# A two-layer encoder: the second layer's output projection as seven products of quarters

## The chip, the core and the metric

The kernel runs on one NeuronCore of a Trainium2 chip. Its time is the device time of one execution, in microseconds, as the median of several runs. A core has a matrix engine (PE, with its weight loads as PEld), a vector engine (DVE), a scalar engine (ACT), a general engine (POOL) and a queue engine (SP); SP, ACT and POOL issue DMAs. Each engine works through its own list of instructions in the order of that list.

## The reference

A trunk of two layers over 512 tokens of width 1024, all in float32. Each layer is a mixer with a gated branch, a residual add, and a gated per-layer embedding; layer 0's mixer is attention over a neighbourhood, layer 1's is dense attention with low-rank queries and keys. Cut to what matters here:

```python
def mixer_mla(xn, w_in, q_norm, w_qb, kv_norm, w_kvb, w_out):
    ...
    o = block_attention(q, k, v)
    return (o.reshape(B, S, H * MLA_V) * jax.nn.silu(z)) @ w_out

def reference(x, p, ...):
    for i in range(DEPTH):
        xn = rmsnorm(x, norm_g[i])
        ...
        h = x + y
        gate = jax.nn.sigmoid(rmsnorm(h, ple_norm[i]) @ ple_w_gate[i])
        x = h + gate * (p[i] @ ple_w_proj[i])
    return rmsnorm(x, final_norm)
```

The change is about `(o * silu(z)) @ w_out` and `h = x + y` of layer 1: 512 x 1024 times 1024 x 1024.

## The kernel before

**Precision.** Every float32 operand of a product is kept as two parts, a rounded `hi` (an ACT copy) and the remainder `lo` (a subtraction on POOL or DVE), and a product is hi·hi + lo·hi + hi·lo: three matmuls of 128 rows, 128 columns of stationary operand and up to 512 moving columns. A weight piece is 128 x 1024; `load_w` (L72) loads it into one of three `wraw` buffers on SP's queue, and makes `hi` and `lo` of it.

**Stages.** The first layer's attention (`na_heads`, L224), its output projection and gate; then the second layer's compression (`mla_c`, L669) with its gate projections z (`z_phase`, L164: eight weights, each 24 matmuls, `Silu` into the eight tiles `zs`), its heads (`mla_heads`, L717), its output projection (`out_proj`, L414) and its gate (`gate_seven`, L564). The loop in `run` (L1009) does projection and gate of both layers.

**Heads.** A loop of 70 steps i, four to a head, interleaves on PE: the scores of step i (`score`), whose softmax goes over DVE, ACT and POOL; the transposes of step i-3 (`turn`); the products with the values of a head before (`output`); and pieces of work for later (`pieces`, L856), among them the per-layer embedding's products (`ple`, L896), 16 calls of 3 matmuls, whose results are stored on SP. When a pair of heads j is done, `half_of` joins it (DVE, L205) and `gated` (L207) multiplies by `zs[j]` (POOL, L209) and splits the result into `oT`, the projection's operand.

**The output projection.** `out_proj` loads eight pieces of `mla_o`; per column half n and row tile t, 24 matmuls add up in one PSUM bank; DVE adds it to the residual row (L427), and `turn_h` (L1023) then scales the row (`hg`, DVE, L1028), transposes it (PE) and gives it to `keep_half` (L536), which makes operands X of the gate's products. The residual rows (`r`, from `spill`) and the norm's gains (`gp`) are read at the beginning of this stage. The framework may place its matmuls from step 53 of the heads on.

**The gate, already from seven products.** `gate_seven` cuts both operands in quarters (256 tokens x 512 features, 512 x 512 weights) and forms 7 products instead of 8, each of two row tiles and 12 matmuls. Sums of quarters of the weights are formed in DRAM by `sum_step` (L518), eight DMAs of 1 MB a layer on POOL's queue, every second one of which adds onto what is there; they are issued one a head during the first layer's attention. The last product, 4, is done in halves of 256 columns at the end.

**Order.** The framework orders each engine's instructions when the program is built, by its own model of their durations, in which the order of the program text is the priority; `issue_after(x)` puts an instruction behind x on the same engine. A buffer pool hands out a tile when an old one's last reader is done. PSUM has eight banks here (tags mm 2, S 2, T 3, O 1, L67).

## Time and profile before

| | us |
|---|---|
| median of 3 runs | 661.84 (661.47 to 661.88) |
| the profiled execution | 662.75 |
| its span, first to last instruction | 660.6 |

The mean granted clock of TensorE in it was 0.997. The rows in the next section are of that one execution: a line of code, an engine, an operation, what it writes and reads, how often, and either start and duration (timelines), or total and mean (groups); in brackets the idle time before it and what ended that. In a row of a stretch the first number is its length, and each engine's busy time follows. The chain is the work that ended last, followed back.

### The profile page before, as it was taken

What the parts mean: (1) busy time and instruction counts of PE and PEld (TensorE: products, weight loads), DVE (VectorE), ACT (ScalarE), POOL (GpSimd) and SP (SyncE); (2) the same over time, 40 slices, a digit from 0 to 9 for tenths busy, and PEclk for the clock granted to TensorE, in tenths of its full rate; (3) what the DMA queues carried; (4) which work ended last, traced back from release to release, by engine and by line L of the source; (5) the groups of instructions that cost most, each with busy time, mean ns of one, the idle gap of its engine ahead of it and who ended that gap; (6) DMA issues with size and microseconds to landing.
All of it is one profiled execution on the core that took longest, in us unless ns stands there. A gap on an engine that the chain in (4) does not pass through costs nothing.

```text
span 660.6 us, 10121 instructions
## 1 busy us (share of the span) xinstructions
PE 648.1 (98%) x3419; PEld 550.8 (83%) x3419; DVE 403.3 (61%) x856; ACT 439.4 (67%) x875; POOL 432.5 (65%) x381
## 2 busy tenths in 40 slices
PE   9999999999999999999999999999999999999994
PEld 6888888988988888887899888888888888888884
DVE  6190365836546526568833623888888876474865
ACT  7672586856767743787643535888979897537945
POOL 0495485686685674687555525795959878436974
PEclk9999999999999999999999999999999999999998
DMA  9944357886587779445733344220211213584524
GB/s 326 346 144 147 96 168 190 221 201 143 172 218 173 199 172 372 161 132 167 250 90 105 106 109 141 65 75 3 64 56 65 66 59 133 202 308 128 166 90 159
DMA packets 44755, 102.18 MB, mean 155 GB/s; under 512 B 4640, under 2 KB 17696, under 8 KB 44704
## 3 DMA queue, kind: packets, MB, share of 16 engines
q1 hardware_dynamic: 33776, 83.97, 38.3%
q0 software_dynamic: 10496, 16.78, 11.8%
q10 hardware_dynamic: 432, 0.79, 0.3%
q8 instruction: 27, 0.44, 0.3%
q14 instruction: 24, 0.20, 0.1%
HBM read 89.99 MB, written 25.17 MB: 174 GB/s over the span
## 4 chain that ended last, share of the span: by engine, by line
PE 87%; DVE 3%; DMA 3%; POOL 2%; ACT 2%; issue 2%; POOLq 0%; ACTq 0%; DVEq 0%
PE ps_mm L107 33%; PE ps_S L107 13%; PE ps_mm L734 6%; PE ps_T L139 5%; PE ps_O L845 4%; PE ps_T L637 4%; PE ps_T L107 3%; PE ps_O L107 3%; PE ps_T L238 2%; PE ps_S L637 2%; PE ps_O L400 2%; PE ps_mm L637 2%; PE ps_mm L184 2%; DMA sum<-gate 1%; PE ps_T L388 1%
## 5 line engine op out<-in xcount | busy, mean ns | idle before, releaser
L84 POOL TENSOR_TENSOR wwlo<-wraw,wwhi 128x1024 fp32r<-128x1024 f32 (+5 forms) x78 | 142.8, 1845 | 73.1 <-ACT wwhi L83 52.4
L83 ACT ACTIVATE wwhi<-wraw 128x1024 fp32r<-128x1024 f32 (+5 forms) x81 | 65.5, 832 | 53.7 <-issue 19.7
L585 POOL TENSOR_TENSOR wlo<-wraw,whi 128x512 fp32r<-128x512 f32 x56 | 74.0, 1352 | 24.5 <-ACT whi L583 19.7
L830 POOL TENSOR_TENSOR ex<-ex,rc 128x512 f32<-128x512 f32 x64 | 66.1, 1042 | 25.4 <-DVE rc L829 18.1
L828 ACT ACTIVATE ex<-ps_S,mx 128x512 f32<-128x512 f32 x64 | 44.0, 688 | 12.2 <-DVE mx L826 11.1
L826 DVE TENSOR_REDUCE mx<-ps_S 128x1 f32<-128x512 f32 x64 | 43.7, 683 | 7.2 <-PE ps_S L107 6.8
L96 DVE TENSOR_TENSOR pt_lo<-ps_T,pt_hi 128x512 fp32r<-128x512 f32 x64 | 43.3, 682 | 7.7 <-ACT pt_hi L94 7.3
L374 POOL TENSOR_TENSOR ex<-ex,rc 128x128 f32<-128x128 f32 (+1 forms) x64 | 36.0, 634 | 14.6 <-DVE rc L370 14.6
L94 ACT ACTIVATE pt_hi<-ps_T 128x512 fp32r<-128x512 f32 x64 | 37.8, 595 | 4.3 <-PE ps_T L139 4.1
L107 PE MATMUL ps_mm<-xh,wwhi 128*128 128x512 f32 x152 | 40.3, 398 | 0.0
L107 PE MATMUL ps_mm<-xl,wwhi 128*128 128x512 f32 x152 | 38.5, 391 | 0.0
L139 PE MATMUL ps_T<-ident,ex 128*128 128x128 f32 x256 | 38.4, 272 | 0.0
L107 PE MATMUL ps_mm<-xh,wwlo 128*128 128x512 f32 x152 | 38.2, 391 | 0.0
L139 PEld LDWEIGHTS ps_T<-ident,ex 128*128 128x128 f32 x256 | 31.4, 140 | 7.7 <-POOL ex L830 0.4
L107 PEld LDWEIGHTS ps_mm<-xh,wwlo 128*128 128x128 f32 x152 | 28.3, 188 | 6.0
L107 PEld LDWEIGHTS ps_mm<-xl,wwhi 128*128 128x128 f32 x152 | 28.3, 188 | 5.8
L205 DVE TENSOR_TENSOR u<-ps_O,u 64x512 f32<-64x512 f32 x32 | 22.0, 687 | 17.2 <-ACT u L204 16.7
L583 ACT ACTIVATE whi<-wraw 128x1024 fp32r<-128x1024 f32 x28 | 29.3, 1056 | 4.9 <-DMA wraw<-sum 2.7
L209 POOL TENSOR_TENSOR u<-u,z 128x512 f32<-128x512 f32 x16 | 21.8, 1361 | 15.6 <-DVE u L205 9.1
L368 ACT ACTIVATE ex<-ex,mx 128x128 f32<-128x128 f32 (+1 forms) x64 | 30.3, 475 | 2.0 <-DVE mx L358 1.1
L107 PEld LDWEIGHTS ps_mm<-xh,wwhi 128*128 128x128 f32 x152 | 27.3, 188 | 4.8
L107 PE MATMUL ps_S<-ke,qe 96*128 96x512 f32 x96 | 29.1, 408 | 0.4 <-DMA qe<-rl 0.4
(432 smaller groups left out, 1848.1 us busy)
## 6 DMA issues: line engine op xcount, KB each, us to landing
sum<-gate POOLq DMA_DIRECT2D x12, 1024.0 KB, 8.1
wraw<-na_qk SPq DMA_DIRECT2D x16, 512.0 KB, 3.4
wraw<-sum SPq DMA_DIRECT2D x16, 512.0 KB, 3.3
pe<-pe SPq DMA_DIRECT2D x31, 256.0 KB, 6.8
wraw<-gate SPq DMA_DIRECT2D x12, 512.0 KB, 3.4
wraw<-na_v SPq DMA_DIRECT2D x8, 512.0 KB, 4.1
sum<-sum POOLq DMA_DIRECT2D x4, 1024.0 KB, 9.3
wraw<-na_o SPq DMA_DIRECT2D x8, 512.0 KB, 4.2
```

Source lines behind the costliest of these rows:

```text
L83: nc.scalar.activation(hi[:, c], raw[:, c], AF.Copy)
L84: f = lambda e, c=c: e.tensor_tensor(out=lo[:, c], in0=raw[:, c], in1=hi[:, c].bitcast(F32), op=ALU.subtract)
L94: self.last_copy = nc.scalar.activation(hi, src, AF.Copy, scale=scale)
L96: nc.vector.tensor_tensor(out=lo, in0=src, in1=hi.bitcast(F32), op=ALU.subtract)
L107: last = self.last_mm = nc.tensor.matmul(out, l, r, start=i == 0, stop=i == n - 1)
L139: self.last_mm = self.nc.tensor.transpose(t[:, i * P:(i + 1) * P], b, self.ident)
L585: nc.gpsimd.tensor_tensor(out=lo[:, o], in0=raw[:, o], in1=hi[:, o].bitcast(F32), op=ALU.subtract)
L637: mm = nc.tensor.matmul(ps, l, r, start=j == 0 and p in banks, stop=j == 11 and p in (2, 3, 4), skip_group_check=True)
L734: self.last_mm = nc.tensor.matmul(PS[key], *terms[i], start=i == 0, stop=i == len(terms) - 1)
L826: nc.vector.reduce_max(mx, sp, axis=AX.X, negate=True)
L828: nc.scalar.activation(ex, sp, AF.Exp, bias=mx, accum_out=sm)
L830: nc.gpsimd.tensor_tensor(out=ex, in0=ex, in1=rc.to_broadcast([P, S]), op=ALU.mult)
```

## The change

- `gated` becomes `quartered`: the gated head pair is written back into `zs[j]`, and `eighth` splits parts of it into the operands Y of the seven products: product 1 from pairs 0 to 3, products 2 and 4 from pairs 4 to 7. `first_difference` makes product 7's operand in the last eight steps of the heads, `late_quarters` those of 6, 5 and 3 in the output stage.
- `out_seven` replaces `out_proj` in layer 1. Its 7 x 2 x 12 matmuls are strictly chained; each result is added to or subtracted from the residual rows where it belongs, 18 adds on DVE. The order is 1, 7, 2, 4, 6, 5, 3; products 2, 4, 5, 3 add onto the bank of 1, 7, 6, 6. It may start after step 66 (`LAST`) instead of 53.
- `ring_weight` loads the fourteen weight pieces of this stage and of both gates, into places by a list of letters; DVE takes some of the `lo` parts: the second piece of layer 1's projection for all products but 1 and 7, and of its gate for products 1, 7 and 2.
- Eight more `sum_step` DMAs make the quarter sums of `mla_o`: four in the first layer's attention, at heads 2, 6, 10 and 14 behind that head's own, and four in the second layer's z stage, behind the `lo` of z's weights 0, 2, 4 and 6.
- The four residual rows and the gains are read at step 60 of the heads, into the place of `cT`, which is done then.
- The embedding's stores go from SP's queue to ACT's, and one of its calls comes before step 64 instead of at 67.
- Layer 1's gate takes its products in the order 1, 7, 6, 2, 5, 3, 4, and `keep_half` makes the operands of 5 and 3 there as soon as it can.

```diff
     def half_of(self, u, O, e):
...
+    def quartered(self, u, zs, X, j):
+        z, l, r = zs[j], slice(0, 256), slice(256, 512)
+        self.nc.gpsimd.tensor_tensor(out=z, in0=u, in1=z, op=ALU.mult)
+        if j < 4:
+            self.eighth(X, 1, j, z[:, l])
+        else:
+            self.eighth(X, 2, j - 4, z[:, l])
+            self.last_gate = self.eighth(X, 4, j - 4, z[:, r])
+    def first_difference(self, X, zs, j):
+        z, l, r = zs[j], slice(0, 256), slice(256, 512)
+        with self.tc.issue_after(self.last_norm.ins):
+            self.nc.gpsimd.tensor_tensor(out=z[:, l], in0=z[:, l], in1=z[:, r], op=ALU.subtract)
+        self.eighth(X, 7, j, z[:, l], self.nc.vector)
+    def late_quarters(self, X, zs):
...
+        for j in range(4):
+            z, w = zs[j], zs[4 + j]
+            sub(z[:, l], z[:, l], w[:, r], ALU.add)
+            self.eighth(X, 6, j, z[:, l], self.nc.vector, self.last_copy)
...
+    def eighth(self, X, p, k, x, lo=None, after=None):
+        if p not in X:
+            X[p] = self.bigtile(f"Y{p}").rearrange("p a (b c) -> p (a b) c", b=2)
+        t = X[p]
+        with self.tc.issue_after(after.ins) if after else nullcontext():
+            self.nc.scalar.activation(t[:, k, :], x, AF.Copy)
+        return (lo or self.nc.gpsimd).tensor_tensor(out=t[:, 4 + k, :], in0=x, in1=t[:, k, :].bitcast(F32), op=ALU.subtract)
...
+        def sums(h):
+            l, step = divmod(h, 8)
+            self.sum_step(l, step)
+            if h % 4 == 2:
+                self.sum_step(2, h // 4)
...
+    def ring_weight(self, pool, layer, p, c, after=None):
+        place = "oobbobwwwwwooo" if layer == 2 else "ooowwwwwooowww"
...
+        vector = c and (layer == 2 and p not in (1, 7) or layer == 1 and p in (1, 7, 2))
+        for o in (slice(0, S), slice(S, 2 * S)):
+            with self.tc.issue_after(self.last_half.ins) if layer == 2 and vector else nullcontext():
+                (nc.vector if vector else nc.gpsimd).tensor_tensor(out=lo[:, o], in0=raw[:, o], in1=hi[:, o].bitcast(F32),
+                                                                   op=ALU.subtract)
+    def out_seven(self, pool, Y, zs, res, after, mm):
+        order = (1, 7, 2, 4, 6, 5, 3)
...
+        for k, p in enumerate(order):
+            if k + 3 < 7:
+                prep(order[k + 3])
+            if k == 0:
+                self.late_quarters(Y, zs)
+            for i in range(2):
...
+                for j, (l, r) in enumerate(m):
+                    with self.tc.issue_after(mm if j == i == 0 and p == 1 else mm.ins):
+                        mm = nc.tensor.matmul(ps, l, r, start=j == 0 and p in banks, stop=j == 11 and p in (2, 3, 4),
+                                              skip_group_check=True)
+                if p == 1:
+                    add(i, 1, ps, ALU.subtract)
+                    add(2 + i, 0, ps)
+                    add(2 + i, 1, ps, ALU.subtract)
...
+                elif p == 2:
+                    add(i, 0, ps)
+                    after(i, 0)
...
@@ mla_heads
-            nc.sync.dma_start(self.pe[1][t][:, n * S:(n + 1) * S], o)
+            nc.scalar.dma_start(self.pe[1][t][:, n * S:(n + 1) * S], o)
+        def sums(j):
+            if j % 2 == 0:
+                with self.tc.issue_after(self.last_rest.ins):
+                    self.sum_step(2, 4 + j // 2)
-        zs = self.z_phase(a["mla_z"], xT, range(NEARLY))
+        zs = self.z_phase(a["mla_z"], xT, range(NEARLY), also=sums)
...
-            if i == 53:
+            if i == LAST:
                 last = self.last_mm
+            if i == 60:
...
+                for t in range(NT):
+                    nc.sync.dma_start(res[t], self.spill[t])
```

## The prediction

> **What bounds the kernel now.** I read the page first (span, busy shares, chain), then the busy time by stage, then the waits of PE.

> ```profile
> span 660.6 us, 10121 instructions
> ...
> PE 648.1 (98%) x3419; PEld 550.8 (83%) x3419; DVE 403.3 (61%) x856; ACT 439.4 (67%) x875; POOL 432.5 (65%) x381
> ...
> PE 87%; DVE 3%; DMA 3%; POOL 2%; ACT 2%; issue 2%; POOLq 0%; ACTq 0%; DVEq 0%
> ```

> The program's span is 660.6 us of an execution of 662.75, so 2.15 lie around it. PE is busy for 98% of the span and carries 87% of the chain that ended last: work taken from PE shortens the kernel, as long as the other engines can still feed it. A busy share is an average, so here are the stages: first attention, the second layer's gate projections (z), its heads, its output projection, its gate products.

> ```profile
> core 0: us, PE busy (x) PEld busy (x) DVE busy (x) ACT busy (x) POOL busy (x), PEclk, DMA share, GB/s
> 69.00:259.00 190.00, 188.82 (x1100) 166.03 (x1099) 101.62 (x305) 125.53 (x276) 126.36 (x120) 1.00 0.72 192
> ...
> 347.00:412.00 65.00, 65.00 (x336) 55.94 (x335) 26.49 (x74) 31.02 (x63) 32.01 (x25) 1.00 0.38 114
> 412.00:560.00 148.00, 147.62 (x812) 123.71 (x811) 122.49 (x247) 127.07 (x282) 118.45 (x110) 1.00 0.21 65
> 560.00:613.00 53.00, 53.00 (x252) 44.00 (x252) 28.42 (x35) 28.82 (x43) 26.67 (x20) 1.00 0.57 205
> 613.00:652.00 39.00, 39.00 (x197) 33.12 (x195) 29.02 (x47) 27.29 (x49) 32.52 (x27) 1.00 0.38 128
> ```

> The first number after the comma is PE's busy time. In the output stage, 560 to 613, it is the whole 53.00 us, while DVE, ACT and POOL are each busy for about half. That stage is bound by its matmuls alone. After the last matmul comes a tail that the change doesn't touch: both kernels end on product 4 in halves.

> ```profile
> 651.63 0.40 PE L637 MATMUL ps_O<-wlo,X 128*128 128x256 f32 x2
> ```

> **The matmuls (on the path).** The old projection is 2 halves x 4 row tiles x 24 matmuls = 192. The new one is 7 products x 2 row tiles x 12 = 168, of the same shape (128 rows, 512 columns). The chain has stretches of such matmuls back to back:

> ```profile
> 597.47 5.49 PE ps_T L107 x24
> ...
> 630.12 16.32 PE ps_T L637 x72
> ```

> 16.32 / 72 = 0.227 us each, so 24 fewer are **-5.44 us**. Transposes and the gate's matmuls stay equal in number.

> [...] The trace shows 227 ns at full clock here; the measurement decides, and the sum goes by it.

> **The end of the heads.** The old kernel may lay output matmuls between the heads' last steps; the new one only after step 66 (LAST), so of the cover only the per-layer embedding's matmuls remain, one of them a step earlier.

> ```profile
> 557.88 2.04 POOL L830 TENSOR_TENSOR ex<-ex,rc 128x512 f32<-128x512 f32 x2
> ...
> 559.52 0.71 PE L107 MATMUL ps_S<-wwhi,o1h 128*128 128x512 f32 x2
> ...
> 564.87 0.60 PE L139 MATMUL ps_T<-ident,ex 128*128 128x128 f32 x4
> ...
> 568.53 1.07 PE L845 MATMUL ps_O<-pt_hi,vt 128*128 128x512 f32 x4
> ```

> From 559.52 to 564.87 the old kernel ran 7 output matmuls, 1.6 us: the price if all of them covered a real wait. POOL's last softmax products were done at 557.88 + 2.04 = 559.9, and without the 7 their transposes come at 564.87 - 1.6 = 563.3, so I take 0.3 (bounds 0 and 1.6). Added in these steps: four `first_difference` (POOL, ACT, DVE on 128x256), the four residual reads and two gain reads on SP at step 60, and the embedding's stores, which leave SP for ACT:

> ```profile
> 656.53 0.38 ACTq L1103 DMA_DIRECT2D out<-r  x1
> ```

> Eight such issues are 3 us on ACT's queue, where the next exp stands behind each. ACT is 86% busy in the heads (127.07 of 148), so they fit. What SP wins: its weight loads no longer stand behind stores that wait for data. The residual reads cost nothing, having the heads over them; without that cover they would lie where they do now, in a stage whose PE never waits.

> **The start of the output stage.** Product 1 may use the scratch of the embedding's operands only after the last embedding matmul. Then its second weight piece needs an ACT copy and two POOL halves.

> ```profile
> L585 POOL TENSOR_TENSOR wlo<-wraw,whi 128x512 fp32r<-128x512 f32 x56 | 74.0, 1352 | 24.5 <-ACT whi L583 19.7
> ...
> L583 ACT ACTIVATE whi<-wraw 128x1024 fp32r<-128x1024 f32 x28 | 29.3, 1056 | 4.9 <-DMA wraw<-sum 2.7
> ```

> That is 1.06 + 2 x 1.35 = 3.8 us. Before it, PE has 6 matmuls of the first piece (1.4) and the last head's 8 (1.8), and 4 more of the second piece need only the copy (0.9): 4.1 against 3.8. I take 0.3 (0 to 1.5, if the copy queues behind the last probability copies).

> **The output stage's side work (beside PE, if it fits).** Fourteen weight pieces replace eight; each feeds 12 matmuls (2.7 us) instead of 24.

> ```profile
> L84 POOL TENSOR_TENSOR ww<-wraw,ww 128x1024 fp32r<-128x1024 f32 x2 | 5.1, 2565 | 6.3 <-ACT ww L83 6.3
> ...
> L84 DVE TENSOR_TENSOR wwlo<-wraw,wwhi 128x1024 fp32r<-128x1024 f32 x1 | 1.2, 1226 | 0.3 <-ACT wwhi L83 0.3
> ...
> L427 DVE TENSOR_TENSOR r<-ps_mm,r 128x512 f32<-128x512 f32 x3 | 2.1, 692 | 3.3 <-PE ps_mm L107 3.3
> ...
> 636.22 0.43 DVE L618 TENSOR_TENSOR ps_S<-ps_S,s 128x256 f32<-128x256 f32 x1 [1.96 <-ACT s L649]
> ...
> 94.67 0.61 POOL L374 TENSOR_TENSOR ex<-ex,rc 128x256 f32<-128x256 f32 x1
> ```

> The stage shrinks to 53 - 5.4 = 47.6 us. DVE: 28.4, plus 10 more adds into the residual (18 for 8) at 0.69 = 6.9, plus 12 remainders of the late quarters at 0.43 = 5.2, five weight remainders for four (+1.2), product 5's operand made earlier (2 x 0.69): 43.1, or 91%. POOL: 26.7, less three old pieces (7.5), plus eight new at 2.7 (21.6), plus 12 quarter sums at 0.61 to 0.65 (7.5), less two pieces of the gate that DVE takes over (5.4): 42.9, or 90%. ACT: 28.8 plus six copies (6.3) and 12 at about 0.4: 40, or 84%. The heads, at 83%, 86% and 80% (122.49, 127.07, 118.45 of 148), leave PE 0.4 us idle, and the gate stage runs POOL at 83% under a full PE. So 90% can be carried, with less room. The added waits: product 5 adds onto product 6's bank and product 3 onto product 5's, so PE waits for DVE's add, behind which `turn_h` and `keep_half` queue, and PE's transposes wait for those; two tiles alternate, so an add has 2.7 us for its 0.69. I take 0.5 (0 to 5, the upper end in the first rival).

> **The eight DMAs that sum `mla_o`'s quarters (POOL).** Four are issued in the first attention and four in the z stage. What such a DMA costs POOL, and what waiting for one costs PE, shows here:

> ```profile
> L522 POOL DMA_DIRECT2D sum<-gate x12: 801/952/1323, 88.8 to 225.0; - x12
> ...
> sum<-gate POOLq DMA_DIRECT2D x12, 1024.0 KB, 8.1
> ...
> sum<-sum POOLq DMA_DIRECT2D x4, 1024.0 KB, 9.3
> ...
> 124.77 0.80 POOL L522 DMA_DIRECT2D sum<-gate  x1
> ...
> 134.61 1.31 POOL L522 DMA_DIRECT2D sum<-sum  x1 [6.18 <-DMA sum<-gate]
> ...
> 137.64 0.33 PE L386 MATMUL ps_T<-ident,ex 128*128 128x128 f32 x1 [0.28 <-POOL ex L374]
> ...
> 138.20 0.44 PE L388 MATMUL ps_T<-ident,ex 128*128 128x128 f32 x2 [0.24 <-POOL ex L374]
> ...
> 139.78 0.35 PE L400 MATMUL ps_O<-ph,vt 128*128 128x192 f32 x1 [0.67 <-DVE u L205]
> ```

> At 134.61 POOL sat 6.18 us for the landing of the DMA issued at 124.77; the softmax factors stood behind it, and PE lost 0.28 + 0.24 + 0.67 = 1.2 us. The change puts one more transfer ahead of that one, at head 2. The queue has room there (the next old one comes a head later), so I take 0.6 for this stage (0 to 4: a hold longer by half a landing, 8.1 / 2, us for us). In the z stage:

> ```profile
> 356.79 7.15 POOL L84 TENSOR_TENSOR wwlo<-wraw,wwhi 128x1024 fp32r<-128x1024 f32 x3 [3.58 <-ACT wwhi L83]
> ...
> 365.17 1.06 POOL L123 TENSOR_TENSOR rs<-ss,half 128x1 f32<-128x1 f32 x2 [1.23 <-DVE ss L118]
> ...
> 366.29 2.62 DVE L128 SCALAR_TENSOR_TENSOR cn<-c,rs,gkv 128x256 f32<-128x256 f32 x1
> ...
> 369.57 0.82 PE L139 MATMUL ps_T<-ident,cn 128*128 128x128 f32 x6
> ```

> Behind a sum DMA stand the weight remainders and the norm's power (L123); the transposes at 369.57 wait for what follows it, and that ends at 366.29 + 2.62 = 368.91. The slack is 0.66 us, less than one issue (0.95). I take 0.3 (0 to 5).

> **The sum**, against the profiled execution: -5.44 + 0.3 + 0.3 + 0.5 + 0.6 + 0.3 = -3.4, or 662.75 to 659.3. The median shown is 661.84, 0.9 below that execution; the same difference makes **658.4**.

> **Rivals.** *DVE and POOL become the bound of the output stage.* For it: 91% and 90%, and the slow row below. Against: ten microseconds of DVE time are free in the gate stage behind it (29.02 of 39), to which product 6's and 3's operands can slip.

> ```profile
> 588.58 0.75 DVE L1028 SCALAR_TENSOR_TENSOR hg<-r,rowb,gp 128x512 f32<-128x512 f32 x1
> ...
> 615.60 1.85 DVE L1028 SCALAR_TENSOR_TENSOR hg<-r,rowb,gp 128x512 f32<-128x512 f32 x1
> ...
> 609.34 10.53 POOL L585 TENSOR_TENSOR wlo<-wraw,whi 128x512 fp32r<-128x512 f32 x8
> ```

> The same DVE operation took 0.75 us alone and 1.85 within a row of POOL subtractions. The change adds 12 remainders on DVE with both inputs in SBUF, and as many sums on POOL: at +1.1 for about eight of them DVE needs 43.1 + 8.8 = 52 of 47.6 us, 4.3 too much: 658.4 + 4.3 - 0.5 = 662.2 if none of it slips, 660.1 if half does. Centre **661.2**. [...]

> *Slower: POOL is held by its own DMAs.* Place: the first attention and the z stage. Price: a transfer ahead of the one awaited at 134.61 pushes its landing by up to 4, and PE has nothing left there, so 4; in the z stage POOL splits three z weights in 7.15 us, so two z's are about 5 us apart, a landing takes 8.1, and an accumulating DMA holds POOL 3.1, less 0.66 of slack 2.5, for each of two sums: 5. Together 9: 661.84 - 5.44 + 9 = **665.4**. It decides from 6.7 us of such waits on (5.44 + 1.3). For it: the 6.18. Against: all other holds of POOL on these DMAs together are 0.3 us, as the row of their sum shows.

> ```profile
> POOL sum L522 <- DMA sum<-gate: 6.5, 2, 6.2
> ```

> *The saving doesn't appear*: the strict order of products, each on its own weights, makes PE wait as long as it saves (an order in which one late piece stops PE, where the old projection had other tiles to turn to): **661.8**.

> **Chances.** Forecast 0.55 (656.4 to 660.2); no new wait at all, under 656.4: 0.07; first rival 0.20; POOL held 0.14; no saving 0.04. Two in ten may be left out: from 656.0 to 663.6. A measurement of this kernel can tell about 0.2%, 1.3 us: faster (under 660.5) is 0.55 + 0.07 + a quarter of the first rival = 0.67; same, to 663.2, the rest of it and no saving = 0.19; slower 0.14.

> **What would show it.** PE should have 24 matmuls fewer, at 0.227; its last matmul should start near 651.63 - 3.4 = 648.2 and the tail stay 9 us. The forecast holds if PE's new waits sum to about 2 us; the first rival shows as PE waiting for DVE or POOL remainders after product 2; the second as POOL holds on `sum` of over 6 us and PE waits behind them at 110 to 145 or 360 to 390. Wrong would be a PE wait in a stage not named here, or matmuls that take longer.

## The result, and the profile after

The changed kernel took a median of 681.07 us (679.73 to 682.06, 4 runs) beside 661.86 us (661.47 to 662.85, 4 runs) of the kernel before in the same session: a ratio of 1.029 [1.026, 1.031]. It is 19 us slower; 3.4 us faster was forecast.

From the page of its profile: the span, PE's row, the software DMA queue (packets, MB, share of 16 engines) and the chain.

```profile
span 678.5 us, 10187 instructions
...
PE 651.4 (96%) x3395; PEld 549.4 (81%) x3395; DVE 440.2 (65%) x894; ACT 449.4 (66%) x901; POOL 466.3 (69%) x417
...
q0 software_dynamic: 15744, 25.17, 17.4%
...
PE 72%; DVE 9%; DMA 8%; POOL 5%; ACT 3%; issue 2%; SPq 0%; POOLq 0%; ACTq 0%; DVEq 0%
```

Before, the software DMA queue carried 10496 packets and 16.78 MB (11.8%). PE has exactly 24 matmuls fewer (3395 for 3419), yet is busy 3.3 us longer, and its share of the chain fell from 87% to 72%. The new waits of PE, longest first (us in total, times, longest):

```profile
PE ps_T L142 <- DVE hg L1183: 3.3, 1, 3.3
PE ps_T L142 <- DVE cn L131: 2.7, 1, 2.7
PE ps_mm L110 <- DVE vt L99: 2.0, 1, 2.0
PE ps_T L775 <- DVE a L689: 1.9, 1, 1.9
PE ps_S L638 <- ACT a L694: 1.9, 1, 1.9
PE ps_S L638 <- POOL wlo L599: 1.1, 2, 0.7
PE ps_S L638 <- DVE r L618: 0.8, 1, 0.8
```

`hg`, `r`, `a` and `wlo` belong to the output and gate stages, `cn` to the z stage, `vt` to the first attention. The busy times by stage, answering to those before (first attention; z; heads; projection; gate):

```profile
69.00:259.00 190.00, 187.24 (x1086) 163.16 (x1085) 105.81 (x302) 123.92 (x274) 130.43 (x123) 1.00 0.79 204
350.00:418.00 68.00, 65.17 (x328) 55.37 (x326) 30.81 (x73) 29.07 (x61) 35.51 (x28) 0.97 0.63 167
418.00:571.00 153.00, 152.62 (x837) 128.30 (x838) 126.64 (x254) 131.35 (x295) 122.55 (x121) 1.00 0.27 85
571.00:625.00 54.00, 46.93 (x208) 36.94 (x207) 45.09 (x59) 29.44 (x48) 40.15 (x35) 0.97 0.52 169
625.00:669.00 44.00, 41.40 (x200) 34.61 (x199) 33.37 (x55) 33.10 (x57) 37.24 (x29) 0.96 0.44 146
```

In the projection PE is idle for 7.1 of 54 us, while DVE is busy for 45.1. The last three columns are the granted clock, the DMA share and GB/s: in three stages the clock is below 1.00. Windows of 3.41 us around four of the waits show why:

```profile
374.26:377.67 3.41, 0.78 (x5) 0.74 (x6) 2.73 (x5) 0.41 (x1) 3.01 (x2) 1.00 1.23 185
377.67:381.08 3.41, 3.41 (x9) 2.65 (x9) 2.63 (x11) 1.42 (x7) 1.08 (x2) 0.50 1.05 311
592.71:596.12 3.41, 0.85 (x4) 0.36 (x2) 3.41 (x5) 0.72 (x2) 3.41 (x4) 1.00 0.21 43
596.12:599.53 3.41, 2.71 (x9) 2.33 (x10) 3.41 (x4) 1.98 (x4) 3.41 (x4) 0.50 0.30 115
637.08:640.49 3.41, 1.48 (x9) 1.08 (x7) 3.38 (x7) 3.01 (x6) 3.41 (x4) 1.00 0.45 154
640.49:643.90 3.41, 3.41 (x10) 2.64 (x9) 3.41 (x5) 1.36 (x3) 3.29 (x2) 0.50 0.48 154
138.74:142.15 3.41, 2.29 (x11) 1.94 (x12) 1.18 (x3) 3.38 (x9) 3.41 (x6) 1.00 1.22 189
142.15:145.57 3.42, 3.42 (x21) 2.97 (x20) 1.12 (x2) 2.31 (x4) 3.42 (x5) 1.00 1.14 284
```

After a window in which PE was busy for 0.78, 0.85 or 1.48 us, the next 3.41 us run at a granted clock of 0.50; after one with 2.29 us they do not. Three such stretches lie ahead of the last matmul (from 377.67, 596.12 and 640.49). Each costs up to half its length, 1.7 us: less where PE also waits in it, as in the second, in which it is busy for 2.71 us. A fourth, from 671.21, lies behind the last matmul, where the kernel before has one too (from 656.02).

The table splits the profiled executions at starts of PE's matmuls: the first on `x1h` (second layer), the first scores of its heads, the last product with values, the first gate product, the last matmul, the span's end. The first column is everything before the first of these. Ratios are those of all runs to the kernel before on the same chip.

| kernel | first layer | compression, z | heads | projection | gate | tail | ratio [95%] |
|---|---|---|---|---|---|---|---|
| before | 325.4 | 84.3 | 160.4 | 42.9 | 38.7 | 8.9 | 1 |
| after | 328.5 | 88.7 | 159.1 | 48.5 | 43.5 | 10.2 | 1.029 [1.026, 1.031] |
| e1 sums alone | 333.1 | 88.8 | 161.0 | 42.9 | 38.7 | 8.9 | 1.019 [1.017, 1.022] |
| e9 tiny sums | 323.8 | 86.6 | 160.2 | 42.9 | 38.7 | 8.9 | 1.003 [1.002, 1.005] |
| e2 no sums | 324.1 | 84.3 | 158.2 | 48.3 | 42.9 | 10.2 | 1.016 [1.014, 1.017] |
| e8 one on DVE | 329.0 | 87.8 | 162.5 | 49.9 | 42.5 | 10.1 | 1.035 [1.031, 1.040] |
| e3 no late lo | 331.0 | 89.5 | 159.2 | 44.1 | 43.3 | 10.2 | 1.026 [1.022, 1.029] |
| e4 no late sums | 331.2 | 87.7 | 159.2 | 46.7 | 42.6 | 10.3 | 1.027 [1.024, 1.030] |
| e5 sums in heads | 323.8 | 84.3 | 164.2 | 48.8 | 42.9 | 10.2 | 1.022 [1.020, 1.024] |
| e6 late turns | 324.0 | 84.3 | 163.7 | 49.6 | 45.7 | 9.5 | 1.028 [1.026, 1.029] |
| e7 sums on DVE | 323.5 | 84.3 | 162.1 | 47.8 | 42.2 | 10.2 | 1.019 [1.017, 1.022] |
| e12 slots | 324.6 | 84.3 | 162.0 | 48.9 | 43.3 | 10.2 | 1.020 [1.019, 1.022] |
| e10 light | 324.1 | 84.3 | 158.3 | 41.8 | 42.5 | 10.2 | 1.003 [1.002, 1.004] |
| e11 lighter | 324.5 | 84.3 | 158.2 | 41.5 | 44.7 | 10.1 | 1.004 [1.002, 1.005] |
| e13 gate order (e7) | 324.9 | 84.3 | 163.8 | 47.7 | 44.8 | 9.6 | 1.024 [1.022, 1.025] |
| e14 gate order (e10) | 324.5 | 84.3 | 158.2 | 42.9 | 46.1 | 9.5 | 1.008 [1.006, 1.010] |
| e15 no mixed lo | 324.4 | 84.3 | 158.2 | 42.1 | 40.8 | 10.2 | 1.0012 [1.0000, 1.0023] |
| e16 no DVE weights | 324.2 | 84.3 | 158.2 | 42.2 | 40.6 | 10.2 | 1.0005 [0.9996, 1.0014] |

After minus before, unrounded: 3.05 + 4.43 - 1.27 + 5.62 + 4.72 + 1.30 = 17.85 us, as the spans say (678.5 - 660.6).

### The profile page after: what moved, and what is told of

It reads as the page before. It is cut to its first block, busy times and chain, and to the rows that moved or that the text cites. A ratio compares the mean times of both kernels' runs of the same rounds, so it can differ in the third digit from the quotient of the medians.

```text
span 678.5 us, 10187 instructions
## 1 busy us (share of the span) xinstructions
PE 651.4 (96%) x3395; PEld 549.4 (81%) x3395; DVE 440.2 (65%) x894; ACT 449.4 (66%) x901; POOL 466.3 (69%) x417
## 4 chain that ended last, share of the span: by engine, by line
PE 72%; DVE 9%; DMA 8%; POOL 5%; ACT 3%; issue 2%; SPq 0%; POOLq 0%; ACTq 0%; DVEq 0%
PE ps_mm L110 23%; PE ps_S L110 11%; PE ps_mm L872 6%; PE ps_T L142 5%; PE ps_T L775 5%; DMA sum<-gate 5%; PE ps_O L983 4%; PE ps_T L110 3%; PE ps_T L291 2%; PE ps_O L110 2%; PE ps_mm L187 2%; POOL wlo L599 1%; DVE X L678 1%; POOL ex L433 1%; PE ps_S L775 1%
## 5 line engine op out<-in xcount | busy, mean ns | idle before, releaser
L85 POOL TENSOR_TENSOR wwlo<-wraw,wwhi 128x1024 fp32r<-128x1024 f32 (+5 forms) x76 | 140.7, 1886 | 58.7 <-ACT wwhi L84 32.8
L599 POOL TENSOR_TENSOR wlo<-wraw,whi 128x512 fp32r<-128x512 f32 x64 | 90.2, 1437 | 22.8 <-ACT whi L595 17.8
L84 ACT ACTIVATE wwhi<-wraw 128x1024 fp32r<-128x1024 f32 (+5 forms) x78 | 62.3, 822 | 53.0 <-issue 20.5
L595 ACT ACTIVATE whi<-wraw 128x1024 fp32r<-128x1024 f32 x39 | 41.1, 1058 | 14.2 <-DMA wraw<-gate 5.2
L99 DVE TENSOR_TENSOR pt_lo<-ps_T,pt_hi 128x512 fp32r<-128x512 f32 x64 | 43.3, 682 | 6.7 <-ACT pt_hi L97 6.5
L210 DVE TENSOR_TENSOR u<-ps_O,u 64x512 f32<-64x512 f32 x32 | 22.0, 687 | 22.2 <-ACT u L209 21.6
L427 ACT ACTIVATE ex<-ex,mx 128x128 f32<-128x128 f32 (+1 forms) x64 | 30.3, 475 | 4.8 <-DVE mx L417 3.3
L775 PE MATMUL ps_T<-whi,X 128*128 128x512 f32 x96 | 27.2, 404 | 2.6 <-DVE a L689 1.9
## 6 DMA issues: line engine op xcount, KB each, us to landing
sum<-gate POOLq DMA_DIRECT2D x12, 1024.0 KB, 9.4
sum<-mla_o POOLq DMA_DIRECT2D x6, 1024.0 KB, 10.0
sum<-sum POOLq DMA_DIRECT2D x6, 1024.0 KB, 10.5
```

Of the source, the lines that this page charges most:

```text
L84: nc.scalar.activation(hi[:, c], raw[:, c], AF.Copy)
L85: f = lambda e, c=c: e.tensor_tensor(out=lo[:, c], in0=raw[:, c], in1=hi[:, c].bitcast(F32), op=ALU.subtract)
L99: nc.vector.tensor_tensor(out=lo, in0=src, in1=hi.bitcast(F32), op=ALU.subtract)
L595: nc.scalar.activation(hi, raw, AF.Copy)
L599: (nc.vector if vector else nc.gpsimd).tensor_tensor(out=lo[:, o], in0=raw[:, o], in1=hi[:, o].bitcast(F32), op=ALU.subtract)
L775: mm = nc.tensor.matmul(ps, l, r, start=j == 0 and p in banks, stop=j == 11 and p in (2, 3, 4), skip_group_check=True)
```

## The experiments

**Theories.** A: the eight sum DMAs cost PE time in the first attention and the z stage (by their place, A1, or by their transfer, A2). B: in the output stage DVE's instructions with two SBUF inputs and POOL's work stand in one line, and that line is late (before, one `hg` took 0.75 us alone and one 1.85 within a row of POOL subtractions). Rivals: C, the strict order of products; D, DVE overfull by its own count.

### The sum DMAs: e1, e9, e2, e8

e1, the kernel before with the DMAs alone:

```diff
+            if h % 4 == 2:
+                self.sum_step(2, h // 4)
...
+        zs = self.z_phase(a["mla_z"], xT, range(NEARLY), also=sums)
```

> The kernel before with the eight DMAs that sum mla_o's quarters added at the places where the changed kernel has them; nothing reads their results. Theory A (the DMAs delay POOL's and DVE's small steps in the first attention and in the z stage, and PE waits there): PE loses what the changed kernel lost up to the heads, +3.4 us before 250 us and +4.7 us in the z stage, about 670 us, and the granted clock shows one stretch of 3.4 us at half rate after the z stage's wait. Rival (what was predicted, 0.6 + 0.3 us; the loss comes from the other edits): 662.8 us.

Measured 674.13 us, +13: theory A, and more than it said. The excess lies in the first layer (+7.6) and the z stage (+4.5); from the heads on hardly anything changed (+0.6 in the heads). Its profile has two half-clock stretches ahead of the last matmul, one of them already in the first attention, at 163.2.

e9, the same DMAs with 2 rows each:

```diff
+        n = 2 if layer == 2 else 2 * P
+        self.nc.gpsimd.dma_start(self.sums[layer][p][0:n], src[0:n],
```

> The kernel before with the eight added DMAs of the first experiment at the same places, but each moves 2 rows of 4 KB instead of 256 (8 KB instead of 1 MB); nothing reads their results. Theory A1 (what costs is their place in POOL's order, their issue and what the framework reorders around them): most of the first experiment's +13 us stays, 668 us or more, with the same wait for cn in the z stage. Theory A2 (what costs is the transfer: 8 MB more beside the weight loads, later landings of the DMAs that POOL awaits): 661 to 664 us.

Measured 663.17 us. POOL's order is that of e1 throughout (the other engines' nearly so: DVE's differs in the place of two instructions, ACT's of one, PE's of about a dozen); with 8 KB instead of 1 MB, the first layer costs nothing more (323.8 for 325.4 before). There it is the transfer, A2. How long POOL stood at its own accumulating DMAs in the first attention (us, times, longest), in e9, in e1 and after:

```profile
POOL sum L534 <- DMA sum<-gate: 6.8, 3, 5.5
```

```profile
POOL sum L533 <- DMA sum<-gate: 14.5, 4, 7.6
```

```profile
POOL sum L666 <- DMA sum<-gate: 13.3, 4, 7.1
```

Before it was 6.5. In the z stage 2.3 us of the 4.5 stay with tiny transfers (86.6): that part is the place, A1. The rows before, POOL alone:

```profile
366.20 2.42 POOL L84 TENSOR_TENSOR wwlo<-wraw,wwhi 128x1024 fp32r<-128x1024 f32 x1
369.87 2.40 POOL L84 TENSOR_TENSOR wwlo<-wraw,wwhi 128x1024 fp32r<-128x1024 f32 x1 [1.25 <-ACT wwhi L83]
```

The rows after, POOL first, then DVE, then PE:

```profile
369.39 1.09 POOL L126 TENSOR_TENSOR rs<-ss,half 128x1 f32<-128x1 f32 x2 [1.56 <-DVE ss L121]
370.44 1.37 POOL L666 DMA_DIRECT2D sum<-sum  x1
371.30 5.24 POOL L85 TENSOR_TENSOR wwlo<-wraw,wwhi 128x1024 fp32r<-128x1024 f32 x2
```

```profile
370.53 6.31 DVE L131 SCALAR_TENSOR_TENSOR cn<-c,rs,gkv 128x256 f32<-128x256 f32 x1
```

```profile
376.89 0.55 PE L142 MATMUL ps_T<-ident,cn 128*128 128x128 f32 x3 [2.66 <-DVE cn L131]
```

The norm's factor `rs` was there by 370.5. DVE's `cn` began during the issue of the DMA and ended at 376.84, just behind POOL's run of that issue and two remainders (371.30 + 5.24 = 376.54). Before, POOL paused 1.25 us between those two remainders (ahead of 369.87), and `cn`, begun at 366.29, ended in that pause, after one of them. In e9 the same `cn` took 5.78 us, and PE waited for it nearly as long:

```profile
371.39 0.55 PE L141 MATMUL ps_T<-ident,cn 128*128 128x128 f32 x3 [2.11 <-DVE cn L130]
```

By these rows the transfer's part of the 4.4 us after is 0.5 us of longer wait (2.66 for 2.11) and the half-clock stretch from 377.67, up to 1.7 us. e9 has no such stretch there: its wait falls across two windows, in which PE is still busy for 2.72 and 2.00 us.

e8, one of the two remainders on DVE:

```diff
-            w = first if first and j == js[0] else self.load_w(wap[j], 1024)
+            w = first if first and j == js[0] else self.load_w(wap[j], 1024, rest=nc.vector if also and j == 3 else None)
```

> The changed kernel with the lo of z's weight 3 on DVE instead of POOL; the sum DMAs stay where the change puts them. Theory B (the norm's cn on DVE stood 6.3 us behind a DMA issue and two remainders of POOL in a row): with one remainder less in that row cn is ready 2.4 us or more earlier, PE's wait of 2.7 us in the z stage goes, and the stretch at half clock behind it too: 676 to 678 us. Rival (POOL itself is held by the landing of a sum DMA there): unchanged, 680 to 681 us.

Measured 684.96 us, a miss in the time, but the step in question did what theory B says:

```profile
371.07 1.22 DVE L85 TENSOR_TENSOR wwlo<-wraw,wwhi 128x1024 fp32r<-128x1024 f32 x1 [0.66 <-ACT wwhi L84]
372.21 0.61 DVE L131 SCALAR_TENSOR_TENSOR cn<-c,rs,gq 128x384 f32<-128x384 f32 x1
372.74 0.48 DVE L131 SCALAR_TENSOR_TENSOR cn<-c,rs,gkv 128x256 f32<-128x256 f32 x1
```

`cn` took 0.48 us, and PE's wait for it is gone. In its place PE waited 3.1 and 1.7 us at the first scores, at 416.8 and 419.7, with 6.8 us at half clock. The first of these waits is counted in the z stage; without it that stage takes 84.7 us, about what it took before (84.3). The last sum DMA landed 12.7 us after its issue (388.19 to 400.94) and z's last weight, beside it, 8.1 us (392.48 to 400.60; 3.6 is the median before). That these late loads are what the scores waited for was not tried by itself.

e2, the changed kernel without the DMAs:

```diff
-            if h % 4 == 2:
-                self.sum_step(2, h // 4)
...
-        src = self.quarter[layer][p] if p < 4 else self.sums[layer][p]
+        src = self.quarter[layer][p] if p < 4 else self.sums[min(layer, 1)][p]
...
-        zs = self.z_phase(a["mla_z"], xT, range(NEARLY), also=sums)
+        zs = self.z_phase(a["mla_z"], xT, range(NEARLY))
```

> The changed kernel without those eight DMAs: products 4 to 7 of the projection take the sums of the second gate's weights instead of mla_o's, so these four products are formed with other weights of the same shape. Theory A: first attention and z stage as in the kernel before, 681.1 - 8 = 673 us; the output stage and the gate keep their waits. Rival (the DMAs only moved a wait that appears again at the heads' end): about 680 us.

Measured 671.16 us: theory A. First layer and z stage are back; projection, gate and tail keep their excess, which is therefore a thing of its own.

### The output stage: e3, e4, e6, e7

In `eighth` (e3, whose matmuls then read the `hi` part) and in `late_quarters` (e4):

```diff
+        if p in (3, 5, 6):
+            return None
```

```diff
-                pool.tensor_tensor(out=out, in0=x, in1=y, op=op)
+                pass
```

> The changed kernel without the 12 remainders (lo) of the operands of products 6, 5 and 3, which are DVE's; their matmuls read the hi part in their place, as many as before. Theory B (DVE is late in the output stage, because its instructions with two SBUF inputs stand in one line with POOL's): the 12 took about 10 us of DVE there; hg is ready some 4 us earlier, PE's waits of 3.3, 1.9 and 0.8 us and one or two stretches at half clock go: about 673 us. Rival C (the strict order of products and their late weight pieces hold PE): no change, 680 to 681 us.

> The changed kernel without POOL's 12 sums and differences of quarters in the output stage (products 6, 5 and 3 take the quarters unsummed); DVE's work stays as it is. Theory B (DVE and POOL exclude each other): DVE's remainders of the quarters shrink from about 0.9 to 0.42 us and its first hg of the stage comes 3 to 5 us earlier, 674 to 677 us. Rival D (DVE is only overfull by its own count, POOL has room): no change, 680 to 681 us.

Both totals, 678.28 and 678.65 us, fell by under 3 us, a miss in size, and by their intervals they can't be told from the changed kernel's. One reason: in the profiled runs the first layer was 2.5 and 2.7 us longer than in the changed kernel's (a wait of 3.6 us at 123, and a half-clock stretch behind it, which that one lacks). The projection itself shrank by 4.4 and 1.9 us (in e3 its half-clock stretch is gone too). C, which allowed neither, falls; e4 took work from POOL alone and still shortened DVE's instructions, against D. DVE's remainders and `hg` in the projection (total, mean ns), after:

```profile
L266 DVE TENSOR_TENSOR Y<-z,Y 128x256 fp32r<-128x256 f32 x12 | 10.6, 912 | 0.0
...
L1183 DVE SCALAR_TENSOR_TENSOR hg<-r,rowb 128x512 f32<-128x512 f32 x6 | 7.7, 1282 | 0.1
```

and in e4, without POOL's 12 sums:

```profile
L266 DVE TENSOR_TENSOR Y<-z,Y 128x256 fp32r<-128x256 f32 x12 | 8.3, 746 | 0.0
L1183 DVE SCALAR_TENSOR_TENSOR hg<-r,rowb 128x512 f32<-128x512 f32 x7 | 6.3, 905 | 0.2
```

The next kernels have the DMAs in the heads (e5):

```diff
+            if i % 6 == 4 and i < 52:
+                with self.tc.issue_after(self.last_norm.ins):
+                    self.sum_step(2, i // 6)
```

> The changed kernel with its eight sum DMAs moved from the first attention and the z stage into the second layer's heads, one every sixth step from step 4 to 46. Theory A (the DMAs cost only where POOL and DVE have no slack): first attention and z stage as in the kernel before, heads unchanged, about 671 us, as without the DMAs. Rival (POOL is 80% busy in the heads, and eight issues of about 1.1 us hold up the softmax factors): the heads lose 3 us or more, 674 us or more.

Measured 675.72 us: the rival's number. First layer and z are back to before, but the heads are 6.0 us longer than without the DMAs (164.2 against 158.2), though not by POOL's softmax factors:

```profile
PE ps_S L110 <- DMA qe<-rl: 3.7, 2, 3.0
```

PE waited for moves of rotated queries; the one of the long wait (`qe<-rl`, issued at 479.56) landed after 4.8 us beside a sum DMA issued at 476.42, and a half-clock stretch followed. e12 (below) puts them elsewhere.

e6 binds the transposes of `hg` one to one and a half products later:

```diff
-                    after(i, 0)
+                    later(i, 0)
...
+                for x in [x for x in pend if x[0] == 2 * k + i]:
+                    self.pin = mm
+                    after(*x[1:])
```

> As the one with the sums in the heads, and PE's transposes of hg are bound behind matmuls one to one and a half products later, so that DVE has 3 us more for each. Theory B (DVE is late by its stretched instructions, but not overfull): the wait of 3.3 us at the first transposes, the stretch at half clock after it and part of the later ones go, 4 to 6 us off the kernel with the sums in the heads, 665 to 667 us. Rival D (DVE is the bound of the stage): the waits only move to later matmuls and transposes, less than 2 us off.

Measured 679.28 us, slower than e5:

```profile
PE ps_S L640 <- ACT a L703: 4.2, 1, 4.2
PE ps_T L784 <- ACT a L716: 3.4, 1, 3.4
...
PE ps_T L142 <- DVE hg L1190: 1.0, 1, 1.0
```

The wait for `hg` shrank from 3.2 to 1.0 us and the waits behind it grew by more. So "late, but not overfull" isn't borne out. That the stage has more side work than time is not shown by this alone, since the edit also hands the gate its rows later; e10 below shows it.

e7 moves the 12 sums of quarters from POOL to DVE:

```diff
-            with self.tc.issue_after(self.last_gate.ins):
-                pool.tensor_tensor(out=out, in0=x, in1=y, op=op)
+            with self.tc.issue_after(self.last_half.ins):
+                self.nc.vector.tensor_tensor(out=out, in0=x, in1=y, op=op)
```

> As the one with the sums in the heads, with the 12 sums and differences of quarters of the output stage on DVE in place of POOL. Rival D (DVE overfull by its own count): 5 us more on DVE, the output stage 3 to 5 us longer. Theory B (one line for DVE's instructions with two SBUF inputs and POOL's): the line loses POOL's 9 us and gains 5, the stage is equal or up to 3 us shorter, and DVE's remainders of quarters come nearer to 0.42 us.

Measured 674.43 us, e5's 675.72 or a little under. DVE got 12 instructions more, and the projection was 1.1 us shorter (47.8; in e12, with the same projection, 48.9, so equal or a little shorter); D, which wanted 3 to 5 us more, falls. The remainders came down to 452 ns:

```profile
L244 DVE TENSOR_TENSOR z<-z 128x256 f32<-128x256 f32 x12 | 8.0, 714 | 0.0
...
L266 DVE TENSOR_TENSOR Y<-z,Y 128x256 fp32r<-128x256 f32 x12 | 5.0, 452 | 0.0
```

e12 is e7 with the DMAs away from the queries' moves:

```diff
-            if i % 6 == 4 and i < 52:
+            if i == 0 or i % 8 == 5 and i < 60:
```

> As the one with the 12 sums on DVE and the sum DMAs in the heads, with these at step 0 and at steps 5, 13, 21, 29, 37, 45 and 53, away from the steps in which the rotated queries are moved (their landing held PE for 2.6 us at 484 us). Theory A: the heads return to 158 to 160 us and the stretch at half clock there goes: 669 to 671 us. Rival (a sum DMA delays other moves wherever it stands): 673 to 675 us.

Measured 674.68 us, the rival. The wait at 484 went, others came (1.7 us at 557, and 5.5 us in all for the adds in the projection). No place tried for the DMAs was free.

### What is left without the side work: e10, e11, and the gate: e13 to e16

e10 is e2, e3 and e4 together; e11 also returns `hi, hi` for the projection's pieces whose `lo` DVE makes.

> The changed kernel without the sum DMAs (products 4 to 7 take the second gate's sums), without the 12 remainders on DVE and without the 12 sums on POOL (products 6, 5 and 3 take unsummed quarters and their hi part twice); the number of matmuls stays. Theory B (the shared line of DVE and POOL bounds the output stage, and the gate's waits are its backlog): the output stage shrinks from 48.3 to 42 us or less, the gate from 42.9 to 41 or less: 662 to 665 us. Rival C (strict order): 668 us or more.

> As the one before, and the five weight remainders of the output stage that DVE makes are left out too (those pieces use their hi part twice). Theory B: hardly any wait is left in the output stage, 39 to 41 us, and the 24 matmuls saved show at last: 657 to 661 us. Rival C (the strict order of products keeps PE waiting): 666 us or more.

e10: 663.35 us, as B said; the projection is 41.8 us, 6.5 less than in e2. But the gate stayed at 42.5, which B as "backlog" did not allow, and e11, 663.57 us where 657 to 661 were expected, got no further. Heads and projection of e10 together are 200.1 us, 3.2 under the kernel before: there the saving shows. The gate (+3.8) and the tail (+1.3) take it back. In e10 PE waits in the gate once before product 6 and once before a late weight:

```profile
PE ps_T L775 <- DVE a L689: 1.8, 1, 1.8
...
PE ps_S L775 <- POOL wlo L599: 0.7, 1, 0.7
```

e13 and e14 put the gate's old order back, in e7 and in e10:

```diff
-        order = (1, 7, 6, 2, 5, 3, 4) if layer else (1, 7, 2, 6, 5, 3, 4)
+        order = (1, 7, 2, 6, 5, 3, 4)
```

> As the one with the 12 sums on DVE and the sum DMAs in the heads, with the gate's products of layer 1 in the order of the kernel before (1, 7, 2, 6, 5, 3, 4 in place of 1, 7, 6, 2, 5, 3, 4). Theory E (product 6, moved up to the third place, waits for a PSUM bank of the T tag that DVE still reads, since the last rows' transposes come only then): PE's wait of 1.6 to 1.9 us before product 6 goes and the gate shrinks from 42.2 to 39.5 to 40.5 us, 671 to 672.5 us. Rival (the gate's waits are the backlog of the output stage's side work): product 2 waits in its place, no change, 674 us.

> The changed kernel without the sum DMAs, the 12 remainders and the 12 sums of quarters (the light one: products 4 to 7 take the second gate's sums, products 6, 5 and 3 take unsummed quarters and their hi part twice), with the gate's products of layer 1 in the order of the kernel before. Theory E: the gate shrinks from 42.5 to 40 us or less, 660 to 661.5 us. Rival (backlog): 663 us or more, although hardly any backlog is left in it.

676.85 and 666.16 us: the gate grew by 2.6 and 3.6 us, and theory E falls. Product 2 now waits, for its own operand and weight (e13):

```profile
PE ps_mm L773 <- ACT X L675: 1.8, 1, 1.8
PE ps_mm L773 <- DVE wlo L597: 1.1, 1, 1.1
```

So whatever comes third is late. e15 and e16, from e10, take DVE work out ahead of it, in `operand` (p 3 and 5 of layer 1) and in `ring_weight`:

```diff
+        if p in self.skip:
+            return
```

```diff
+        if layer == 1 and vector:
+            return hi, hi
```

> The light kernel (without the sum DMAs, the 12 remainders and the 12 sums of quarters; products 4 to 7 of the projection take the second gate's sums) and in layer 1's gate also without the four remainders (lo) of the operands of products 5 and 3, which read their hi part twice. Theory F (the four last row halves are finished within two products, 2.7 us apart, and DVE and ACT convert each of them in five or six steps; product 6 waits for the end of that burst): PE's wait of 1.8 us before product 6 goes or halves, gate 41 us or less, 661 to 662 us. Rival G (DVE's remainders of the gate's weights are what is in the way): unchanged, 42.5 us, 663.4 us.

> The light kernel, and without DVE's three weight remainders in layer 1's gate (second piece of products 1, 7 and 2: these pieces use their hi part twice). Theory F: DVE saves 3 of these about 5 us before product 6, so the wait shrinks by a part, gate 41.5 us or more. Rival G: the wait before product 6 goes, gate 40.5 us or less, 661 us.

661.74 and 661.73 us; beside their own kernel before that is 1.1 and 1.5 us less than e10, and e15's interval overlaps with e10's. The gate tells more: it is 40.8 and 40.6 us for 42.5, and in both the wait before product 6 is gone. F and G each named one half of it: the two loads of DVE add up, and taking either away is enough. Of the last 2 us of the gate, 1.1 (e15) and 0.4 us (e16) are a wait before product 3; what the rest and the 1.3 us of the tail are was not told apart.

## Why the prediction was wrong

- **Matmuls** (-5.44): right. There are 24 fewer, and once the side work is out (e10) 3.2 us of the saving show in heads and projection.
- **Heads' end and start of the output stage** (0.3 + 0.3): about right for the heads. They took 159.1 us for 160.4, and as 8 output matmuls fewer (10 for 18) lie in them, 1.8 us by count, about 0.5 us of new waits is left. At the start PE waited 1.1 us for product 1's second `wlo`, where 0.3 stood.
- **Side work of the output stage** (0.5): the step that failed is "so 90% can be carried, with less room". Heads and projection were forecast at 198.9 us (203.3 less 5.44, plus 1.1) and took 207.6, 8.7 more. That it is the side work is shown: without the 12 remainders and 12 sums 6.5 us go from the projection (e10 beside e2). The shares of 91% and 90% were counted for DVE and POOL apart, at lone durations; but DVE's instructions with two SBUF inputs took less time when POOL had less work: those of `Y`, 912 ns in the mean, took 746 without POOL's 12 sums (e4) and 452 with these on DVE (e7). The first rival had this, with the place, but priced it at 4.3, not 8.7, and counted on free DVE time in the gate to soften it, while the gate grew too.
- **Sum DMAs in the first attention** (0.6): failed at "the queue has room there". POOL's holds doubled, 6.5 to 13.3 us, and the first layer became 3.0 us longer than before's profile, 4.4 longer than e2's. The hold that the prediction priced grew by 0.9 us alone (7.09 for 6.18); the others, 0.3 us in all before (the prediction's reason against the second rival), became 0.3, 3.2 and 2.7 us (at 179, 226 and 241). That it is the transfer is shown (e9).
- **Sum DMAs in the z stage** (0.3): failed at "the slack is 0.66 us, less than one issue". What counted was not the length of the issue: by the timelines it closed the pause in POOL's run in which `cn` ended before. Measured 4.4, of which e9 gives 2.3 to the place and up to 1.7 are the half clock behind the wait. The second rival, "POOL is held by its own DMAs", had place and size (4 and 5 us; 3.0 and 4.4 measured), and its 6.7 us of further holds were reached in the first attention alone; in the z stage its mechanism was another. It was given 0.14.
- **The gate and the tail**: not in the sum; the tail was said to be one "that the change doesn't touch". They grew by 4.7 and 1.3 us. Of the gate's 4.7, up to 1.7 are a half-clock stretch, and about 1.8 go when DVE's new work there is taken out (e10 to e15 and e16). The rest and the tail stay open.
- **The clock**: no term. Three half-clock stretches of 3.41 us cost up to 5.1 us, which lie in the z, projection and gate rows above.

The first rival came true, the second in the first attention, and the gate on top. I had taken the rivals as alternatives; they lie in different stages and add. The third, that the strict order eats the saving, has little left: with the side work out, heads and projection take 200.1 us, 1.1 more than forecast.

## What to carry to other kernels

Where PE is busy for 98% of the span, a matmul saved must be paid with less side work than it covers: count DVE's instructions with two SBUF inputs and POOL's work as one engine against the time that is left, as the rows of `Y` suggest (912 ns beside POOL's 12 sums, 452 with these on DVE). A DMA that nobody waits for can still cost its bytes, through the loads and accumulations that land later: here in a stage with a DMA share of 0.72 (13.1 us in e1, 1.5 in e9, over the whole kernel), and by e5 and e12 also in the heads, with 0.21, where the transfer was not tried apart from the place. And a wait of PE may bring up to another 1.7 us for the clock: those of 2.66, 3.26 and 1.93 us here were followed by 3.41 us at a granted clock of 0.50, one of 1.97 us was not.
